# Attention generators advanced at one place of each weight chunk instead of two, and the closing spare products taken out

## The chip, the cores and the metric

The kernel runs on one core of one Trainium2 chip. The metric is the device time of one execution in microseconds (us); the time stated for a kernel is the median of several runs. Five engines work on the core side by side, each on its own queue in order: TensorE (PE in the profile; PEld is its weight load), VectorE (DVE), ScalarE (ACT), GpSimd (POOL) and SyncE (SP), which issues most of the DMAs. Products are written to PSUM, which has eight banks in each partition; ACT and DVE read them out.

## The reference

One inference step of a two-layer encoder for two groups of rows, 272 of a new stream (16 learned rows and 256 frames) and 32 of a running one with 128 cached rows. In each layer one projection feeds four mixers on the same normalised rows: A, multi-head latent attention; B, stick-breaking attention; C, differential attention; D, attention on the best keys that an indexer picks. Each mixer's output is projected, weighted by a sigmoid gate, summed and projected again; a squared-ReLU MLP follows.

```python
def _layer(x, ...):
    proj = jnp.einsum('bqd,de->bqe', x, w_in)          # feeds A, B, C, D and the gates
    ...
    score = jnp.einsum('bqh,bqhk->bqk', wi, jax.nn.relu(idx_s))    # D: the indexer
    _, sel = lax.top_k(score, topk)
    ...
    br = jnp.einsum('bqnw,nwd->bqnd', o, w_br)
    g = jax.nn.sigmoid(gates.reshape(bsz, nq, N_BRANCH, D_MODEL))
    mix = jnp.einsum('bqd,de->bqe', jnp.sum(g * br, axis=2), w_out)
    x = _layer_norm(DN_ALPHA * x + mix, ln1_g, ln1_b)
    h = jnp.square(jax.nn.relu(jnp.einsum('bqd,df->bqf', x, w_ff1) + b_ff1))
    x = _layer_norm(DN_ALPHA * x + jnp.einsum('bqf,fd->bqd', h, w_ff2) + b_ff2, ln2_g, ln2_b)
```

## The kernel before

The weights come as one stream of 128 x 1024 blocks in float32. The code calls the work on one block a step; here it is called a chunk. SP loads a block into `raw` (four buffers); `split` (L170) makes two parts of it, `whi` on ACT (L172) and the rest `wlo` (L174) on DVE or, for some chunks, on POOL (three buffers each); PE then makes 24 products of it, eight slices of rows by three (`whi` with `xh`, `whi` with `xl`, `wlo` with `xh`; L301 for the projection chunks, L177 to L179 for the others). A chunk's products are written in two halves of 12 by `st.mm(st, 0)` and `st.mm(st, 1)`. What reads a chunk's result out (`after`) is written at the end of the next chunk.

PE's order is the order in which the code is written. The order of ACT, DVE and POOL is made by a scheduler when the kernel is built. The results lie in two pools of PSUM: four single banks (`bank`, L67) for the chunks' results `fp` and for the small tiles `pw`, `vp`, `td`, `tp`, `uq` and others, and two pairs of banks (`bank2`, L64) for scores and values (`ix`, `sc`, `z`, `av`). The build gives each new tile one of its pool's banks, and the tile waits until the readers of the tile before it in that bank are done.

The attention work is in generators, started when a layer's chunks begin: `lane_v` (L342: value tiles, `vp`), `lane_d` (L513: mixer D's indexer: `pw`, `ix`, `td`, rounds of MAX8 and MATCH_REPLACE on DVE, then its scores), the chain of `lane_c` (L622), `lane_b` (L702) and `lane_a` (L837), and `lane_a0` (L779). The list `active` holds them. Once in a chunk each is advanced by one `next`, and writes a few small products and the work of the other engines behind them. Here the list is split: `lane(0)` advances the generators at even places before the chunk's first 12 products, `lane(1)` those at odd places between the two halves.

Names that come up later: `wiT` is the indexer's weights read out of the projection (L506), and `lane_d` begins with `pw` (L521), made of it. `kiT` (L499 to L502) are the indexer's keys. `BK` (L325, L326) and `gt` (L936) are read-outs of a chunk's `fp`, `VB` (L356, L357) that of a `vp` tile. `SEL` (L579) is the mask that the rounds end in; mixer D's score tiles `s` get it by an addition on POOL (L610) and are taken out of `sc` on DVE (L611). L186 to L188 are three steps of a reciprocal root on DVE. After the last chunk come the sums of the last normalisation (`st`, L1251 and L1253), then 80 products (L1260 to L1272) whose results nothing reads, and then the normalisation and the output.

Of the kernel before, what the change touches and what calls it, by code (L numbers as in the profile page):

```python
# [21 lines left out]
NM, NP, NS, NPAST = 16, 256, 32, 128  # L22
TP = NM + NP
T = TP + NS
# [28 lines left out]
def trunk(ctx: ExitStack, tc, I, O):  # L53
    nc = tc.nc
    PE, ACT, DVE, POOL, SP = nc.tensor, nc.scalar, nc.vector, nc.gpsimd, nc.sync
# [8 lines left out]
    def bank2(name):  # L64
        return ps.tile([128, 2, 512], F32, name=name, tag="at", bufs=2)

    def bank(name):  # L67
        return ps.tile([128, 512], F32, name=name, tag="mm", bufs=4)
# [40 lines left out]
    negb = cst.tile([128, 512], BF16, name="negb")  # L109
    identb = cst.tile([128, 128], BF16, name="identb")  # L110
    xh = cst.tile([128, KT, T + 2], F32R, name="xh")
# [54 lines left out]
    def load(st):  # L166
        st.raw = wp.tile([128, 1024], F32, name="raw", tag="raw", bufs=4)
        SP.dma_start(st.raw, I['w'][st.l, st.c])

    def split(st):  # L170
        st.hi = wp.tile([128, 1024], F32R, name="whi", tag="whi", bufs=3)
        ACT.activation(st.hi, st.raw, AF.Copy)  # L172
        st.lo_t = wp.tile([128, 1024], F32R, name="wlo", tag="wlo", bufs=3)
        st.lo.tensor_tensor(st.lo_t, st.raw, st.hi.bitcast(F32), OP.subtract)  # L174
# [960 lines left out]
    active = []  # L1135
    later = []
    queue = list(steps)
# [57 lines left out]
    def by_block(a, b, half):  # L1195
        for kt in range(4 * half, 4 * half + 4):
            for st in (a, b):
                for k in range(3):
                    st.one(st, kt, k)

    prev, pending = None, []
    for i, st in enumerate(queue):
        if i in first_of:
            l = first_of[i]
            if l:
                late[l] = norm[0]
            active = active + lanes_of[l]
        if i + 4 < len(queue):
            load(queue[i + 4])
        if i + 2 < len(queue):  # L1210
            split(queue[i + 2])

        def lane(k):
            for g in active[k::2]:
                try:
                    next(g)
                except StopIteration:
                    dead.append(g)
        dead = []
        if st.pre:  # L1220
            st.pre()
        both = prev is not None and prev.hold == 2
        lane(0)
        if both:
            by_block(prev, st, 0)
        elif st.hold != 2:
            st.mm(st, 0)
        if prev is not None and prev.hold == 1:
            prev.mm(prev, 1)
        lane(1)  # L1230
        if st.mid:
            st.mid()
        if both:
            by_block(prev, st, 1)
        elif not st.hold:
            st.mm(st, 1)
        active = [g for g in active if g not in dead]
        for f in later:
            f()
        later.clear()  # L1240
        if st.after:
            pending.append((i + st.lag, st))
        while pending and pending[0][0] <= i:
            s = pending.pop(0)[1]
            s.after(s)
        prev = st
    assert not active
    m = norm[0]
    p = [bank("st")[:, m.c0:T] for _ in range(2)]
    for i in (1, 0):  # L1250
        PE.matmul(p[i], ones, m.s[i][:, m.c0:], start=True, stop=False)  # L1251
    for i, last in ((0, m.rk(7)), (1, m.sq)):
        PE.matmul(p[i], ones, last, start=False, stop=True)  # L1253

    lastw, flat, n = queue[-1], xh.rearrange("p k t -> p (k t)"), T - NM
    qa, qb = bank2("qa"), bank2("qb")
    q = [qa[:, 0], qa[:, 1], qb[:, 0], qb[:, 1]]
    hi = lambda i: lastw.hi[:, 128 * (i % 8):128 * (i % 8) + 128]
    for i in range(12):
        PE.matmul(q[0][:, :n], hi(i), xh[:, i % 8, NM:T], start=i == 0, stop=True, skip_group_check=True)  # L1260
    for i in range(12):
        PE.matmul(q[1 + i % 2][:, :n], hi(i), xh[:, i % 8, NM:T], start=i < 2, stop=True, skip_group_check=True)
    for i in range(8):
        PE.matmul(q[3], hi(i), flat[:, 512 * (i % 4):512 * (i % 4) + 512], start=i == 0, stop=True,
                  skip_group_check=True)
    for i in range(24):
        r = slice(64 * (i % 2), 64 * (i % 2) + 64)
        PE.matmul(q[i % 2][:, :n], hi(i)[r], xh[r, i % 8, NM:T], start=i < 2, stop=True, skip_group_check=True)
    for i in range(12):
        PE.matmul(q[2][:, :n], identb, negb[:, :n], start=i == 0, stop=True, skip_group_check=True)  # L1270
    for i in range(12):
        PE.matmul(q[3][0:96, :n], hi(i)[:, 0:96], xh[:, i % 8, NM:T], start=i == 0, stop=True,  # L1272
                  skip_group_check=True)
    m.mu, m.rs = (s[:, m.c0:] for s in m.s)
    v, mm = (e_tile([128, T], k)[:, m.c0:] for k in ("v", "mm"))
    ACT.activation(mm, p[0], AF.Square)
# [6 lines left out]
    for n, kt in enumerate((0, 4, 1, 2, 5, 3, 6, 7)):  # L1283
        m.scale(kt, POOL if kt in (4, 5) else DVE)
        g, b = (vec[:, o + kt:o + kt + 1] for o in (m.g, m.b))
# [135 lines left out]
```

## Time and profile before

| | |
|---|---|
| median of 3 runs | 1102.08 us (1101.89 to 1102.54) |
| the profiled execution's own time | 1101.63 us |
| its span in the profile | 1099.8 us (1.8 us lie around it) |
| PE busy | 1053.5 us, 96% of the span |
| DVE, ACT, POOL busy | 781.8, 604.7, 490.9 us |
| chain of work that ended last | PE 68%, DVE 18%, issue 5%, ACT 4%, POOL 3% |
| granted TensorE clock, mean | 0.99 of full speed |

The profile shows one execution; times in its rows are microseconds from the start of the span. A row of the timeline gives the start, the duration, the engine, the line, the operation, the tile written and the tiles read, the shapes and the count; in brackets, how long the engine was idle before it and which engine, tile and line ended that. PE's products overlap, so the step from one start to the next, not the row's duration, is what a product costs in a row of products. A granted clock of 1.00 is 2.4 GHz and 0.50 is 1.2 GHz.

### The profile page before, as it was taken

How to read it: one execution, taken by the hardware profiler on the slowest of the kernel's cores; microseconds unless marked ns; L12 is line 12 of the kernel's file. 1: busy time of each engine (PE TensorE's matmuls, PEld its weight loads, DVE VectorE, ACT ScalarE, POOL GpSimd, SP SyncE). 2: the span in 40 equal slices, each digit the busy share in tenths (PEclk: the TensorE clock that was granted, in tenths of full speed). 3: DMA queues.
4: the chain of work that ended last, by engine and by line, in shares of the span. 5: the costliest groups of instructions: out<-in, count | busy, mean ns of one | idle time of the engine just before them, and what ended most of it. 6: DMA issues, size and time to landing. Idle time of an engine off the chain costs nothing.

```text
span 1099.8 us, 20415 instructions
## 1 busy us (share of the span) xinstructions
PE 1053.5 (96%) x7906; PEld 998.2 (91%) x7906; DVE 781.8 (71%) x1499; ACT 604.7 (55%) x1067; POOL 490.9 (45%) x359
## 2 busy tenths in 40 slices
PE   7899998999999999999988999899999999999998
PEld 6888887889999899999988888788999989999997
DVE  8948887435798988645578588873468998874444
ACT  5555566556454677533334545675645658763332
POOL 5364555642667632111142644656527683221122
PEclk9999998999999999999998999999999999999999
DMA  7654332334444354544443543333344535454531
GB/s 253 206 181 135 108 125 88 106 109 134 146 142 140 129 173 153 164 161 155 153 156 123 172 121 127 108 103 118 118 155 153 170 115 181 165 173 160 167 135 44
DMA packets 56562, 157.42 MB, mean 143 GB/s; under 512 B 8912, under 2 KB 20624, under 8 KB 56464
## 3 DMA queue, kind: packets, MB, share of 16 engines
q1 hardware_dynamic: 55888, 155.52, 43.4%
q8 instruction: 62, 1.02, 0.4%
q10 hardware_dynamic: 576, 0.59, 0.2%
q14 instruction: 36, 0.29, 0.1%
HBM read 150.02 MB, written 6.07 MB: 142 GB/s over the span
## 4 chain that ended last, share of the span: by engine, by line
PE 68%; DVE 18%; issue 5%; ACT 4%; POOL 3%; DMA 1%; SPq 0%; ACTq 0%; POOLq 0%; DVEq 0%
PE fp L301 23%; PE f L179 11%; PE f L177 11%; PE f L178 11%; DVE wlo L174 3%; POOL r L243 2%; PE av L464 2%; PE br L177 1%; PE br L179 1%; PE br L178 1%; DVE xl L214 1%; DVE xl L259 1%; ACT whi L172 1%; DVE r L1061 1%; DVE v L186 1%
## 5 line engine op out<-in xcount | busy, mean ns | idle before, releaser
L172 ACT ACTIVATE whi<-raw 128x1024 fp32r<-128x1024 f32 x272 | 286.9, 1055 | 267.3 <-PE f L178 112.1
L174 POOL TENSOR_TENSOR wlo<-raw,whi 128x1024 fp32r<-128x1024 f32 x96 | 232.8, 2428 | 219.2 <-ACT whi L172 205.8
L174 DVE TENSOR_TENSOR wlo<-raw,whi 128x1024 fp32r<-128x1024 f32 x176 | 247.9, 1408 | 101.1 <-ACT whi L172 100.7
L301 PE MATMUL fp<-xh,whi 128*128 128x304 f32 (+3 forms) x896 | 283.8, 318 | 11.0 <-DVE u L273 5.1
L301 PE MATMUL fp<-xl,whi 128*128 128x304 f32 (+3 forms) x896 | 272.6, 304 | 6.0 <-DVE xl L259 4.2
L301 PE MATMUL fp<-xh,wlo 128*128 128x304 f32 (+3 forms) x896 | 272.2, 304 | 1.2 <-DVE wlo L1155 0.9
L301 PEld LDWEIGHTS fp<-xh,whi 128*128 128x128 f32 x896 | 171.6, 192 | 28.5 <-issue 22.1
L301 PEld LDWEIGHTS fp<-xl,whi 128*128 128x128 f32 x896 | 172.0, 192 | 9.2 <-DVE xl L259 5.6
L301 PEld LDWEIGHTS fp<-xh,wlo 128*128 128x128 f32 x896 | 171.4, 191 | 2.3 <-DVE wlo L1155 1.5
L179 PE MATMUL f<-xh,wlo 128*128 128x306 f32 (+1 forms) x512 | 155.1, 303 | 5.0 <-DVE wlo L174 4.9
L177 PE MATMUL f<-xh,whi 128*128 128x306 f32 (+1 forms) x512 | 154.4, 302 | 0.0
L178 PE MATMUL f<-xl,whi 128*128 128x306 f32 (+1 forms) x512 | 153.4, 300 | 0.0
L179 PE MATMUL f<-ht,wlo 128*128 128x304 f32 (+1 forms) x512 | 153.1, 299 | 0.0
L177 PE MATMUL f<-ht,whi 128*128 128x304 f32 (+1 forms) x512 | 152.6, 298 | 0.0
L178 PE MATMUL f<-ht,whi 128*128 128x304 f32 (+1 forms) x512 | 152.3, 297 | 0.0
L1049 POOL TENSOR_TENSOR u<-u,nsum 128x304 f32<-128x304 f32 (+1 forms) x64 | 63.5, 996 | 113.3 <-DVE u L273 106.7
L179 PEld LDWEIGHTS f<-xh,wlo 128*128 128x128 f32 x512 | 96.5, 188 | 6.8 <-DVE wlo L174 6.8
L178 PEld LDWEIGHTS f<-xl,whi 128*128 128x128 f32 x512 | 96.9, 189 | 0.1
L177 PEld LDWEIGHTS f<-xh,whi 128*128 128x128 f32 x512 | 96.7, 189 | 0.1
L177 PEld LDWEIGHTS f<-ht,whi 128*128 128x128 f32 x512 | 96.3, 188 | 0.0
L178 PEld LDWEIGHTS f<-ht,whi 128*128 128x128 f32 x512 | 96.2, 188 | 0.0
L179 PEld LDWEIGHTS f<-ht,wlo 128*128 128x128 f32 x512 | 96.2, 188 | 0.0
(328 smaller groups left out, 1801.2 us busy)
## 6 DMA issues: line engine op xcount, KB each, us to landing
raw<-in_w SPq DMA_DIRECT2D x272, 512.0 KB, 3.5
x<-in_x SPq DMA_DIRECT2D x8, 152.0 KB, 4.1
raw<-in_w SPq DMA_DIRECT2D x4, 256.0 KB, 4.5
dscr<-tab SPq DMA_DIRECT2D x4, 167.5 KB
out_y<-r ACTq DMA_DIRECT2D x4, 144.0 KB
out_y<-r SPq DMA_DIRECT2D x4, 144.0 KB, 2.0
bc<-dscr SPq DMA_DIRECT2D x2, 272.0 KB, 3.0
out_dsk<-DK SPq DMA_DIRECT2D x4, 136.0 KB
```

What stands on the lines that cost most here:

```text
L172: ACT.activation(st.hi, st.raw, AF.Copy)
L174: st.lo.tensor_tensor(st.lo_t, st.raw, st.hi.bitcast(F32), OP.subtract)
L177: PE.matmul(out, st.hi[:, wcol], mh, start=start, stop=False)
L178: PE.matmul(out, st.hi[:, wcol], ml, start=False, stop=False)
L179: PE.matmul(out, st.lo_t[:, wcol], mh, start=False, stop=stop)
L186: DVE.scalar_tensor_tensor(v, v, -0.5, y, op0=OP.mult, op1=OP.mult)
L214: DVE.scalar_tensor_tensor(xl[:, kt, c0:T], r, g, xh[:, kt, c0:T].bitcast(F32), op0=OP.mult, op1=OP.subtract)
L243: i = eng.tensor_tensor(self.rk(kt), self.rk(kt), self.mu, OP.subtract)
L259: DVE.scalar_tensor_tensor(xl[:, kt, self.c0:T], self.rk(kt), b, h.bitcast(F32), op0=OP.add, op1=OP.subtract)
L301: PE.matmul(box['p'][:, w], (st.lo_t if k == 2 else st.hi)[:, 128 * kt:128 * kt + 128], (xl if k == 1 else xh)[:, kt, w], start=st.n == 0, ...
L464: PE.matmul(p[64 * half:64 * half + 64, j, a:b], vv, pp, start=i == 0, stop=True, skip_group_check=True)
L1049: POOL.tensor_tensor(u, u, n.rs, OP.mult)
```

## The change

In the main loop, `lane(0)` and `lane(1)` become one loop over all of `active` before the chunk's first half. Nothing is written between the halves any more, save for the few chunks that have a `mid`. The generators themselves, their number of turns and the chunks stay as they are. The 80 products behind the last sums go, with their two pairs of banks.

```diff
-        def lane(k):
-            for g in active[k::2]:
-                try:
-                    next(g)
-                except StopIteration:
-                    dead.append(g)
         dead = []
...
         both = prev is not None and prev.hold == 2
-        lane(0)
+        for g in active:
+            try:
+                next(g)
+            except StopIteration:
+                dead.append(g)
         if both:
             by_block(prev, st, 0)
         elif st.hold != 2:
             st.mm(st, 0)
         if prev is not None and prev.hold == 1:
             prev.mm(prev, 1)
-        lane(1)
         if st.mid:
             st.mid()
...
-    lastw, flat, n = queue[-1], xh.rearrange("p k t -> p (k t)"), T - NM
-    qa, qb = bank2("qa"), bank2("qb")
...
-    for i in range(12):
-        PE.matmul(q[0][:, :n], hi(i), xh[:, i % 8, NM:T], start=i == 0, stop=True, skip_group_check=True)
...
-    for i in range(12):
-        PE.matmul(q[3][0:96, :n], hi(i)[:, 0:96], xh[:, i % 8, NM:T], start=i == 0, stop=True,
-                  skip_group_check=True)
     m.mu, m.rs = (s[:, m.c0:] for s in m.s)
```

On PE, groups of small products that stand between two products of chunks go from 119 to 88 (15 fewer in the first layer, 16 in the second), and those inside a chunk from 43 to 1. The following pieces of the order show three places; the number behind a tile's name tells one tile from another.

PE where `lane_d` begins in the first layer, before the change: `pw` stands in the middle of chunk `fp_728`.

```order
L301 MATMUL fp_728<-xh_84,whi_613 128x304
L301 MATMUL fp_728<-xl_85,whi_613 128x304
L301 MATMUL fp_728<-xh_84,wlo_615 128x304
L521 MATMUL pw_741<-con_73,wiT_677 64x4 x8
L524 MATMUL pw_741<-con_73,wiT_677 32x2 x4
L553 MATMUL ix_757<-kiT_600,DQ_207 64x272 x4
```

The same place with the change (the chunk is now called `fp_753`, the one before it `fp_691`).

```order
L301 MATMUL fp_691<-xh_84,whi_580 128x304
L301 MATMUL fp_691<-xl_85,whi_580 128x304
L301 MATMUL fp_691<-xh_84,wlo_582 128x304
L521 MATMUL pw_728<-con_73,wiT_677 64x4 x8
L524 MATMUL pw_728<-con_73,wiT_677 32x2 x4
L553 MATMUL ix_744<-kiT_600,DQ_207 64x272 x4
L301 MATMUL fp_753<-xh_84,whi_613 128x304
```

`pw` and the first `ix` come 12 products earlier, directly behind the chunk before. In the second layer they move the same way.

PE six and a half chunks later, where a `BK` chunk ends, before the change; `td` stands 12 products further on, in the middle of `fp_1166`.

```order
L301 MATMUL fp_1113<-xl_85,whi_918 128x304
L301 MATMUL fp_1113<-xh_84,wlo_920 128x304
L355 MATMUL vp_1153<-con_73,vf_1145 128x128 x3
L406 MATMUL tp_1162<-con_73,e_872 96x128 x2
L301 MATMUL fp_1166<-xh_84,whi_996 128x304
```

The same place with the change (`fp_1120` for `fp_1113`, `fp_1170` for `fp_1166`).

```order
L355 MATMUL vp_1153<-con_73,vf_1145 128x128 x3
L567 MATMUL td_1162<-acc_931,con_73 128x208
L406 MATMUL tp_1166<-con_73,e_876 96x128 x2
L301 MATMUL fp_1170<-xh_84,whi_996 128x304
L301 MATMUL fp_1170<-xl_85,whi_996 128x304
```

`td` now stands ahead of the chunk. So three single banks are taken between the two chunks instead of two, and the build gives `fp_1170` the fourth, which `fp_1120` has just filled, with six small products between them. Before, `fp_1166` had the bank of a `tp` with 24 chunk products in between. The same happens at `fp_1456`, which gets the bank of `fp_1386`, the chunk before it, read out by `gt` (L936), with 12 small products between. Both places come again in the second layer.

POOL where mixer D's first masks are made, in the first layer, as a piece of the difference.

```order
 L492 TENSOR_TENSOR SEL<-SEL,t_681 32x304
-L174 TENSOR_TENSOR wlo<-raw,whi 128x1024 x20
+L174 TENSOR_TENSOR wlo<-raw,whi 128x1024 x19
 L610 TENSOR_TENSOR s<-bc_98,SEL 128x544
-L174 TENSOR_TENSOR wlo<-raw,whi 128x1024
+L174 TENSOR_TENSOR wlo<-raw,whi 128x1024 x2
```

The first L610 goes ahead of one split of weights; its own place on PE, that of `sc` L382, doesn't move, while the tiles `z` of `lane_b` and their work on ACT and DVE come 12 products earlier. On DVE the order there changes as follows.

```order
L186 SCALAR_TENSOR_TENSOR v_2005<-v_2005,y_2007 128x304
L187 TENSOR_TENSOR v_2005<-v_2005,y_2007 128x304
L611 TENSOR_TENSOR s_2056<-sc_2051,s_2056 128x544
L188 SCALAR_TENSOR_TENSOR y_2007<-v_2005,y_2007 128x304
L389 TENSOR_REDUCE mx_2059<-s_2056 128x2
L725 SCALAR_TENSOR_TENSOR t_1964<-z_1942,t_1964 128x512
```

That was before the change; with it:

```order
L725 SCALAR_TENSOR_TENSOR t_1951<-z_1929,t_1951 128x512
L186 SCALAR_TENSOR_TENSOR v_2005<-v_2005,y_2007 128x304
L611 TENSOR_TENSOR s_2056<-sc_2051,s_2056 128x544
L187 TENSOR_TENSOR v_2005<-v_2005,y_2007 128x304
L389 TENSOR_REDUCE mx_2059<-s_2056 128x2
```

L187 falls behind L611, and the second L725 of `lane_b` goes ahead of it.

## Rows read from the trace of the kernel before

**Rows 1.** The page: busy time of each engine with its share of the span and its instructions, and the chain of work that ended last, by engine.

```profile
PE 1053.5 (96%) x7906; PEld 998.2 (91%) x7906; DVE 781.8 (71%) x1499; ACT 604.7 (55%) x1067; POOL 490.9 (45%) x359
...
PE 68%; DVE 18%; issue 5%; ACT 4%; POOL 3%; DMA 1%; SPq 0%; ACTq 0%; POOLq 0%; DVEq 0%
```

**Rows 2.** The waits of PE over the whole span: the product that waited, then the engine, tile and line that it waited for; microseconds in total, times, the longest.

```profile
PE sc L382 <- DVE s L611: 4.9, 2, 3.1
PE fp L301 <- DVE VB L357: 4.5, 2, 2.3
...
PE rms L786 <- ACT lat L763: 3.2, 1, 3.2
...
PE fp L301 <- ACT PTP L410: 0.8, 1, 0.8
```

**Rows 3.** Stretches of the first layer's attention: the stretch, its length, then busy time and instructions of PE, PEld, DVE, ACT and POOL, the granted clock, the DMA share and GB/s.

```profile
110.00:120.00 10.00, 7.54 (x55) 6.50 (x62) 8.99 (x30) 3.34 (x13) 4.50 (x2) 0.83 0.24 80
120.00:160.00 40.00, 40.00 (x348) 36.33 (x348) 33.48 (x108) 25.45 (x49) 19.37 (x8) 1.00 0.41 130
```

**Rows 4.** The timeline of PE: the first products of two chunks in a row with nothing between them; the first product of a chunk that `vp` follows, and that `vp`; the first of 12 products that `sc` follows, and that `sc`.

```profile
35.42 0.30 PE L301 MATMUL fp<-xh,whi 128*128 128x306 f32 x1
...
38.83 0.30 PE L301 MATMUL fp<-xh,whi 128*128 128x306 f32 x1
...
87.98 0.39 PE L301 MATMUL fp<-xh,whi 128*128 128x304 f32 x1
...
91.42 0.49 PE L355 MATMUL vp<-con,vf 128*128 128x128 f32 x3
...
95.16 0.45 PE L301 MATMUL fp<-xh,whi 128*128 128x304 f32 x1
...
97.08 0.47 PE L669 MATMUL sc<-CK,CBQ 32*64 32x144 f32 x8
```

**Rows 5.** The timeline where `lane_d` begins, first layer: the first product of the chunk in whose middle `pw` stands, a split of weights on ACT, `wiT` on DVE, and `pw`.

```profile
59.04 0.31 PE L301 MATMUL fp<-xh,whi 128*128 128x304 f32 x1
...
59.15 1.06 ACT L172 ACTIVATE whi<-raw 128x1024 fp32r<-128x1024 f32 x1 [0.24 <-issue]
...
60.45 0.47 DVE L506 COPY wiT<-fp 32x304 f32<-32x304 f32 x1 [0.88 <-ACT kiT L501]
...
61.00 0.63 PE L521 MATMUL pw<-con,wiT 32*64 32x4 f32 x16
```

**Rows 6.** The same in the second layer: the chunk's first product, `wiT`, `pw`.

```profile
606.45 0.31 PE L301 MATMUL fp<-xh,whi 128*128 128x304 f32 x1
...
607.87 0.47 DVE L506 COPY wiT<-fp 32x304 f32<-32x304 f32 x1 [1.27 <-ACT kiT L501]
...
608.39 0.63 PE L521 MATMUL pw<-con,wiT 32*64 32x4 f32 x16
```

**Rows 7.** The timeline behind the `BK` chunk, whose last product starts at 91.28: the next chunk's first product on PE, a split of weights and `BK` on ACT, `td` on PE, and the rest of `BK` on DVE.

```profile
92.36 0.41 PE L301 MATMUL fp<-xh,whi 128*128 128x304 f32 x1 [0.23 <-DVE PT L435]
...
92.80 1.04 ACT L172 ACTIVATE whi<-raw 128x1024 fp32r<-128x1024 f32 x1
...
93.75 0.38 ACT L325 ACTIVATE BK<-fp 128x272 f32<-128x272 f32 x1
...
94.85 0.62 PE L567 MATMUL td<-acc,con 128*128 128x208 f32 x2 [0.54 <-ACT PT L433]
...
96.80 0.17 DVE L326 COPY BK<-fp 128x32 f32<-128x32 f32 x1
```

**Rows 8.** The timeline behind the `gt` chunk, whose last product starts at 110.52: the next chunk's first product, `gt` on DVE, and `td` on PE.

```profile
114.23 0.38 PE L301 MATMUL fp<-xh,whi 128*128 128x304 f32 x1 [2.19 <-DVE VB L357]
...
116.17 0.47 DVE L936 TENSOR_SCALAR gt<-fp 128x304 f32<-128x304 f32 x1
...
116.70 0.85 PE L567 MATMUL td<-acc,con 128*128 128x144 f32 x2 [0.27 <-DVE gt L936]
```

**Rows 9.** Two stretches in which the granted clock is 0.50, by the same view and columns as rows 3.

```profile
115.70:119.10 3.40, 3.13 (x13) 2.76 (x12) 3.32 (x10) 0.96 (x5) 2.37 (x1) 0.50 0.23 77
166.90:173.70 6.80, 5.83 (x25) 4.90 (x26) 6.02 (x15) 3.68 (x11) 4.39 (x3) 0.50 0.30 100
```

**Rows 10.** The timeline ahead of the first layer's longest wait: `SEL` on DVE, the addition of `SEL` and a split of weights on POOL, one step of `lane_b` on ACT, two steps on DVE, and the `sc` that waited on PE.

```profile
159.40 0.24 DVE L579 TENSOR_SCALAR SEL<-wk 128x160 f32<-128x160 f32 x1
...
162.49 1.82 POOL L610 TENSOR_TENSOR s<-bc,SEL 128x544 f32<-128x544 f32 x1
...
164.28 2.57 POOL L174 TENSOR_TENSOR wlo<-raw,whi 128x1024 fp32r<-128x1024 f32 x1
164.35 0.65 ACT L724 ACTIVATE t<-t 128x512 f32<-128x512 f32 x1
...
164.68 2.50 DVE L187 TENSOR_TENSOR v<-v,y 128x304 f32<-128x304 f32 x1
...
167.10 0.71 DVE L611 TENSOR_TENSOR s<-sc,s 128x544 f32<-128x544 f32 x1
...
167.87 0.97 PE L382 MATMUL sc<-DK,DQ 64*64 64x208 f32 x8 [3.10 <-DVE s L611]
```

**Rows 11.** The timeline of the end: the last group of the spare products on PE, and the last operation on ACT.

```profile
1093.30 1.84 PE L1272 MATMUL qb<-xh,whi 128*96 128x288 f32 x12
...
1095.54 0.63 ACT L1289 ACTIVATE r<-r,vec 128x288 f32<-128x288 f32 x1 [0.16 <-issue]
```

More of the change, by code (lines that the diff above doesn't have):

```diff
@@ L1253, in trunk @@
         PE.matmul(p[i], ones, last, start=False, stop=True)
-    lastw, flat, n = queue[-1], xh.rearrange("p k t -> p (k t)"), T - NM
-    qa, qb = bank2("qa"), bank2("qb")
-    q = [qa[:, 0], qa[:, 1], qb[:, 0], qb[:, 1]]
-    hi = lambda i: lastw.hi[:, 128 * (i % 8):128 * (i % 8) + 128]
-    for i in range(12):
-        PE.matmul(q[0][:, :n], hi(i), xh[:, i % 8, NM:T], start=i == 0, stop=True, skip_group_check=True)
-    for i in range(12):
-        PE.matmul(q[1 + i % 2][:, :n], hi(i), xh[:, i % 8, NM:T], start=i < 2, stop=True, skip_group_check=True)
-    for i in range(8):
-        PE.matmul(q[3], hi(i), flat[:, 512 * (i % 4):512 * (i % 4) + 512], start=i == 0, stop=True,
-                  skip_group_check=True)
[L1266 to L1271, printed above, removed]
-        PE.matmul(q[3][0:96, :n], hi(i)[:, 0:96], xh[:, i % 8, NM:T], start=i == 0, stop=True,
-                  skip_group_check=True)
     m.mu, m.rs = (s[:, m.c0:] for s in m.s)
```

## The prediction

> **What bounds the kernel now.** I read the page's shares and its chain of waits first: PE is busy for 96% of the span and holds 68% of the chain [rows 1]. So a microsecond that PE neither works nor can work is a microsecond of the result, almost anywhere. Then I asked what PE waits for [rows 2]. What matters here all lies in the two layers' attention, and most of it is ended by DVE: `sc` for L611 (4.9 us), `fp` for `VB` (4.5); `rms` waits 3.2 for ACT. Then the stretches [rows 3]: from 110 to 120 DVE is busy for 8.99 of 10 us and PE for 7.54; from 120 to 160 PE runs without a break (40.00 of 40) with DVE at 33.48; right behind, PE has the longest wait of the layer [rows 10]. So two regimes alternate. Where PE runs through, a saved product or break counts in full. Ahead of a wait that DVE ends, PE only arrives earlier and waits longer, and what counts is when DVE gets there. Last come the stretches at half clock [rows 9]: two of them follow right behind waits of PE, of 2.19 [rows 8] and 3.10 us [rows 10]. Half clock costs more than the wait: a stretch of 3.40 us at 0.50 is worth 1.7 at 1.00, so it loses 1.7; the one of 6.80 loses 3.4. Only the attention and the last 15 us can move, since elsewhere no generator is running.
>
> **The change, part by part.** The sum is made against the profiled execution, 1101.63 us, which is 0.45 under the median of 1102.08.
>
> *Fewer breaks on PE.* There are 31 fewer groups of small products between chunk products. A chunk with nothing between takes 38.83 - 35.42 = 3.41 us, so 12 products take 1.705 [rows 4]. A chunk up to a `vp` takes 91.42 - 87.98 = 3.44, which makes a break worth 0.03; 12 products up to an `sc` take 97.08 - 95.16 = 1.92, which makes it 0.21 [rows 4]. I take the middle, 0.12: 31 x 0.12 = 3.7 us. Nearly all of these breaks lie ahead of one of the waits [rows 2], where the gain is paid only as far as DVE comes earlier too. I count half, -1.9; the bounds are 0 and -31 x 0.21 = -6.5.
>
> *`pw` half a chunk earlier.* In the first layer `pw` now starts at 61.00, and `wiT`, which it reads, ends at 60.45 + 0.47 = 60.92 [rows 5]: nothing is spare. What makes `wiT` late is in the same rows: ACT splits weights at 59.15, just as a chunk ends on PE, and only then reads out the keys that release DVE. The order on ACT and DVE up to there is unchanged, and so is the chunk that they hang on. With the change PE comes to `pw` at 59.04 and must stand until 60.92; the 12 products that filled this time, 61.00 - 59.04 = 1.96, come afterwards. Less a break, that is +1.8. In the second layer it is 608.39 - 606.45 = 1.94, with `wiT` ending at 608.34 [rows 6]: +1.8 again, 3.6 in both.
>
> *The bank of `BK`.* Now the chunk behind the `BK` chunk starts at 92.36 in a bank that was filled long before, and `BK` is read out at leisure: on DVE until 96.97, 5.5 us after its products [rows 7]. With the change that next chunk takes the very bank of `BK`, so it starts when both read-outs are done. ACT splits weights first, into the buffer that the `BK` chunk has just let go (there are three): from 91.5, 1.04 and 0.38 for `BK`, then 0.17 on DVE [rows 7] give 93.1. Without the bank the chunk would start at 92.4: now 92.36, less the wait of 0.23, and a `td` more, 95.16 - 94.85 = 0.31 [rows 4, 7]. So +0.8 at least; at most 96.97 - 92.4 = 4.6, if DVE stays as late as it is. Off that come the 0.23 and 0.54 that are lost there now [rows 7]. DVE has its `BK` right behind `SEL` in the new order, earlier than before, so I take a value near the lower end: +1.0 a layer, 2.0 in both.
>
> *The bank of `gt`.* The same a few chunks on. Now 2.19 + 0.27 us are lost there, and `gt` ends at 116.64 [rows 8], 6 us after its chunk; 1.7 more goes at half clock [rows 9]. With the change the next chunk waits for `gt` instead of `VB`, from 112.0 (114.23 - 2.19); DVE has `gt` behind the last rounds and a `SEL`. Between 113 (everything relaxed) and 118 (as late as now, and one `SEL` later) I find no ground to choose, so I take no change here, with -2 and +4 as bounds for each layer.
>
> The waits for `pw` and `BK`, 5.6 us in both layers, stand ahead of this one, which DVE ends. What DVE does there hangs on PE only in part (it is busy 8.99 of 10). So about half is taken up by it: +2.8, with bounds 0 and +5.6.
>
> *`sc` behind L611.* POOL has L610 one split earlier. `SEL` ends at 159.64 but L610 runs from 162.49 to 164.31 [rows 10]; with POOL free it would end by 161.5. On DVE, L187 (2.50 us, until 167.18, beside POOL's split until 166.85) no longer stands ahead of L611, which starts at 167.10 now. But the second L725 does, and that waits for ACT's L724, which ends at 165.00 [rows 10]. An L725 and an L186 follow before L611; I put them at 1.1 us together (L611 itself, over more columns, takes 0.71 [rows 10]), and at 2.5 if POOL holds one of them as it holds L187 now: L611 starts at 166.1 to 167.5. Since `lane_b` runs 12 products (1.7 us) ahead, L724 may be that much earlier too. I take -1.0 for the first layer; the bounds are -6.5, if the wait goes and with it both half-clock stretches (3.1 + 3.4), and +1.7. In the second layer L187 stays ahead of L611 and an L728 joins it: no change, between -2 and +1.8.
>
> *The rest.* The wait of 0.8 us for `PTP` [rows 2] gets a group of `lane_b`'s products in front of it: -0.4, of 0 to -0.8. `rms` keeps its place and I leave its 3.2 us. The spare products run beside the last normalisation: the products end at 1095.14, ACT's last operation at 1096.17 [rows 11], and nothing reads their banks. Removing them: 0.
>
> The sum: -1.9 + 2.8 + 0 - 1.0 - 0.4 = -0.5, which gives 1101.1 us in the profiled execution and 1101.6 as a median. About 1101.5.
>
> **Rivals.**
> *A. New waits stand where products were (slower).* The mechanism is the read-out just in time: `pw` for `wiT`, and the chunks behind `BK` and `gt`. For it speaks that `wiT` has 0.08 us to spare; against it, that DVE may make PE wait a little later anyway. If nothing is taken up: 3.6 for `pw`, 2 x 1.7 for `BK`, two new half-clock stretches of 1.7 behind waits about as long as the one before 115.7 [rows 8, 9], less 1.9 for breaks: +8.5, 1110 us. It decides from the point where the wait before the chunk behind `gt` is no shorter than 2.2 us.
> The Trainium skill has a rule that speaks for this rival: "Perfetto Trace Analysis", section "Optimizing Tensor Performance", wants independent groups of products to rotate through different PSUM banks, so that reading one out overlaps the next one's products. By that rule both chunks that come back to the bank just filled lose the whole read-out; no run so far shows such a pair here, and 1110 would be its time.
>
> *B. The waits for DVE shrink (faster).* The work of `lane_c`, `lane_d` and `lane_b` starts half a chunk earlier, so DVE and ACT reach L611 earlier. For it: the order on POOL, and the 6.5 us of the 40 ahead in which DVE is idle, with 14.6 of ACT [rows 3]. If the `sc` wait falls by 2.6 and its half clock by 3.4, and `rms` by 1: -7, 1095 us.
>
> *C. It changes nothing.* DVE sets the end of each attention stage whatever PE does: 1102. The order does change in 31 places, so this can only be by absorption.
>
> **How the numbers follow.** Forecast 0.40, by itself 1098 to 1105; A 0.27; B 0.25; C 0.08. A measurement of this kernel can tell 0.2% (2.2 us) from no change, so faster ends at 1099.9 and slower begins at 1104.3. Faster: 0.24 from B and 0.08 from the forecast, 0.32. Slower: 0.26 from A and 0.05 from the forecast, 0.31. Same: 0.37. B by itself spreads from 1090 to 1099 and A from 1105 to 1113, by the bounds above; a range from 1093.5 to 1110 leaves out some 0.08 of B and 0.11 of A.
>
> **What would show it.** Right: `pw` waits about 1.9 us for `wiT` in both layers; the chunk behind `BK` waits 0.8 to 2 for it; the first layer's wait for L611 falls to about 2; from 1083 to the end nothing changes. Wrong: no wait at `pw` (then `wiT` hangs on something else); a half-clock stretch right behind `pw` (A); no half clock behind 160 (B); a chain that ended last with another share of DVE by some points; an end of the program that moves by more than 0.3 us, against the zero for the spare products.

## The result, and the profile after

The changed kernel takes 1118.23 us (median of 4 runs, 1114.0 to 1118.69) against 1101.99 for the kernel before: a ratio of 1.0138 [1.0113, 1.0163], 15 us slower. The profiled execution took 1118.65 us with a span of 1116.8, 17.0 longer than before. The forecast was 1101.5, no change, in a range up to 1110. Three runs further down were slow (1755.8 and 1267.17 us of two experiments, 2015.62 of the kernel before) and count in no ratio.

The page after, busy time and chain, as in [rows 1]:

```profile
PE 1047.2 (94%) x7822; PEld 995.5 (89%) x7826; DVE 788.2 (71%) x1499; ACT 604.3 (54%) x1067; POOL 489.3 (44%) x359
...
PE 67%; DVE 21%; issue 5%; ACT 4%; POOL 3%; DMA 0%; SPq 0%; POOLq 0%; ACTq 0%; DVEq 0%
```

The chain has 3 points more of DVE. PE has less to do (the spare products) and takes longer, so it waits. Its waits after, in the same view as [rows 2]:

```profile
PE sc L382 <- DVE s L611: 3.7, 2, 2.0
...
PE vp L355 <- ACT vf L336: 2.8, 2, 1.4
PE rms L786 <- ACT lat L763: 2.8, 1, 2.8
PE fp L301 <- DVE BK L326: 2.5, 2, 1.3
...
PE fp L301 <- DVE gt L936: 2.4, 2, 1.2
PE tp L406 <- DVE PT L435: 2.2, 2, 1.1
PE pw L521 <- DVE wiT L506: 1.9, 1, 1.9
PE tp L406 <- ACT QA L860: 1.9, 1, 1.9
PE pw L521 <- issue: 1.8, 1, 1.8
...
PE rms L798 <- POOL lat L775: 1.6, 1, 1.6
...
PE tp L406 <- DVE VB L357: 1.5, 2, 0.8
```

The longest waits of before are still there, a little shorter (`sc` 3.7 for 4.9, `rms` 2.8 for 3.2), but for that of `fp` for `VB`, which a `tp` now has (1.5 for 4.5). The other eight lines shown didn't exist before; four of them say "2 times", once in each layer, and `pw` has two lines, one for each layer. Five more of 0.6 to 1.2 us are new further down. All the waits of PE that are longer than 0.2 us come to 53.7 us in the span, against 41.1 before.

The start of the same chunk on PE in both traces shows where this becomes time. Up to the chunk behind `gt` the differences are made at three kinds of place:

| first product of | before | after | later by |
|---|---|---|---|
| chunk that waits for the first normalisation | 31.95 | 34.21 | 2.26 |
| chunk behind the new place of `pw` | 59.04 | 64.58 | 5.54 (of which 1.65 comes back within two chunks, as `ix` moved ahead) |
| chunk behind `BK` | 92.36 | 101.03 | 8.67 |
| chunk behind `gt` | 114.23 | 123.64 | 9.41 |
| output projection, first layer | 316.74 | 324.64 | 7.90 |
| second layer: chunk that waits for the normalisation | 578.55 | 586.50 | 7.95 |
| chunk behind the new place of `pw` | 606.45 | 617.93 | 11.48 |
| chunk behind `BK` | 639.77 | 655.95 | 16.18 |
| chunk behind `gt` | 661.63 | 677.41 | 15.78 |
| output projection | 851.21 | 868.27 | 17.06 |

Behind the chunk behind `gt` the delay swings, between 7.3 and 11.9 us in the first layer and between 13.9 and 19.1 in the second, and ends 1.5 lower and 1.3 higher.

The place behind `BK` in the first layer, in the timeline (compare [rows 7]): PE's three waits in a row, and what ACT and DVE did meanwhile.

```profile
88.80 2.51 DVE L651 SCALAR_TENSOR_TENSOR e<-s,rc 128x272 f32<-128x272 f32 x1
...
92.52 1.26 DVE L562 SCALAR_TENSOR_TENSOR acc<-rl,WI,acc 128x208 f32<-128x208 f32 x1
...
94.82 0.56 DVE L643 TENSOR_REDUCE mx<-s 128x2 f32<-128x416 f32 x1
95.41 0.47 ACT L646 ACTIVATE s<-s,mx 128x208 f32<-128x208 f32 x1 [4.46 <-DVE mx L643]
96.59 0.41 ACT L336 ACTIVATE vf<-fp 128x304 f32<-128x304 f32 x1
97.05 0.55 PE L355 MATMUL vp<-con,vf 128*128 128x128 f32 x3 [1.40 <-ACT vf L336]
98.88 0.41 DVE L435 COPY PT<-tp 112x256 f32<-112x256 f32 x1
99.34 0.42 PE L406 MATMUL tp<-con,e 128*96 128x128 f32 x2 [1.09 <-DVE PT L435]
100.79 0.18 DVE L326 COPY BK<-fp 128x32 f32<-128x32 f32 x1
101.03 0.62 PE L301 MATMUL fp<-xh,whi 128*128 128x304 f32 x1 [1.26 <-DVE BK L326]
```

`vp` waits for `vf`. Nothing is wrong with `vf` itself: on ACT it stands behind the exponentials L646, and ACT stood idle for 4.46 us until DVE had `mx`, which came behind L651 (2.51 us) and the indexer's L562 (1.26). Both ran while POOL made two splits of weights in a row, from 88.63 to 93.55; with POOL idle each took 0.42 on DVE, L562 at 94.12 and L651 at 97.91 (208 columns instead of 272). Before, POOL's splits stood apart here, at 87.88 and 93.92. Whether that pair is what makes `vf` late was not tested. Then `tp` waits for the bank that the `tp` before it has, and the chunk for the bank of `BK`. Each wait is short, and each is ended by a read-out that stands in its queue behind other work.

Behind `gt`, in the same trace (compare [rows 8]), `tp` waits for the bank of `VB` and the chunk for that of `gt`:

```profile
121.82 0.63 PE L406 MATMUL tp<-con,e 128*128 128x128 f32 x4 [0.66 <-DVE VB L357]
123.64 0.41 PE L301 MATMUL fp<-xh,whi 128*128 128x304 f32 x1 [1.20 <-DVE gt L936]
```

The stretches at half clock, in the same view as [rows 9]:

```profile
14.80:18.20 3.40, 3.40 (x15) 3.23 (x13) 2.52 (x7) 1.44 (x3) 1.33 (x3) 0.50 0.84 311
25.00:28.40 3.40, 3.40 (x13) 3.07 (x13) 1.97 (x8) 0.52 (x2) 0.00 (x0) 0.50 0.54 170
100.10:106.90 6.80, 5.88 (x23) 5.88 (x24) 4.29 (x19) 1.73 (x6) 0.55 (x1) 0.50 0.38 119
124.00:127.40 3.40, 3.40 (x16) 3.40 (x15) 2.70 (x14) 0.80 (x4) 1.58 (x1) 0.50 0.51 148
618.90:622.30 3.40, 3.40 (x15) 3.40 (x15) 1.38 (x2) 0.00 (x0) 1.04 (x2) 0.51 0.77 254
656.50:659.90 3.40, 3.40 (x15) 3.40 (x15) 2.92 (x11) 0.34 (x1) 0.00 (x0) 0.50 0.44 118
721.30:724.70 3.40, 3.40 (x16) 3.40 (x16) 3.40 (x4) 2.99 (x7) 3.40 (x3) 0.51 0.40 147
```

In the attention that is 6.80 + 4 x 3.40 = 20.4 us at half clock against 13.6 before (the 10.2 of [rows 9], and one more of 3.4 at 661.8 in the second layer), 3.4 us more lost. The stretch at 618.9 stands right behind `pw`, that at 100.1 behind `BK`. The two at 14.8 and 25.0 stand ahead of every moved product; they make the 2.26 us of the table's first line.

### The profile page after: what moved, and what is told of

Its sections match the earlier page's. It is cut to its first block, busy times and chain, and to the rows that moved or that the text cites. A ratio compares the mean times of both kernels' runs of the same rounds, so it can differ in the third digit from the quotient of the medians.

```text
span 1116.8 us, 20240 instructions
## 1 busy us (share of the span) xinstructions
PE 1047.2 (94%) x7822; PEld 995.5 (89%) x7826; DVE 788.2 (71%) x1499; ACT 604.3 (54%) x1067; POOL 489.3 (44%) x359
## 4 chain that ended last, share of the span: by engine, by line
PE 67%; DVE 21%; issue 5%; ACT 4%; POOL 3%; DMA 0%; SPq 0%; POOLq 0%; ACTq 0%; DVEq 0%
PE fp L301 23%; PE f L179 11%; PE f L177 11%; PE f L178 11%; DVE wlo L174 3%; POOL r L243 2%; PE av L464 1%; PE br L177 1%; PE br L179 1%; PE br L178 1%; DVE wk L576 1%; DVE r L1061 1%; DVE xl L259 1%; DVE xl L214 1%; DVE m L575 1%
## 5 line engine op out<-in xcount | busy, mean ns | idle before, releaser
L301 PE MATMUL fp<-xl,whi 128*128 128x304 f32 (+3 forms) x896 | 276.1, 308 | 5.9 <-DVE xl L259 4.2
L301 PE MATMUL fp<-xh,wlo 128*128 128x304 f32 (+3 forms) x896 | 275.6, 308 | 1.1 <-DVE wlo L1155 1.0
L301 PEld LDWEIGHTS fp<-xh,whi 128*128 128x128 f32 x896 | 174.6, 195 | 26.0 <-issue 15.2
L301 PEld LDWEIGHTS fp<-xl,whi 128*128 128x128 f32 x896 | 175.0, 195 | 9.0 <-DVE xl L259 5.5
L301 PEld LDWEIGHTS fp<-xh,wlo 128*128 128x128 f32 x896 | 174.7, 195 | 2.0 <-DVE wlo L1155 1.5
```

What stands on the lines that cost most here:

```text
L301: PE.matmul(box['p'][:, w], (st.lo_t if k == 2 else st.hi)[:, 128 * kt:128 * kt + 128], (xl if k == 1 else xh)[:, kt, w], start=st.n == 0, ...
```

## The experiments

Ratios are to the kernel before, run on the same chip in the same job; differences in us are the ratio's, at 1102 us.

### The generators alone, and the spare products alone

The first has the changed main loop and the 80 products; the second the loop of before and no spare products.

> The changed kernel with the 80 spare products put back: the move of the generators alone. Theory W (the new waits of PE and the half-clock stretches behind them, all in the attention, make the whole loss): 1114 to 1119 us, like the changed kernel. Theory S (the spare products matter for the clock at the beginning: the changed kernel has half-clock stretches at 14.8 and 25.0 us that the kernel before lacks, 2.3 us lost ahead of any moved product): 1111 to 1116 us, with no half clock before 60 us.

> The kernel before without the 80 spare products, generators at two places as before. Theory W: 1101.5 to 1102.5 us, no change. Theory S: 1103 to 1106 us, with half-clock stretches ahead of 30 us.

Measured: 1117.64 us, ratio 1.0139 [1.0124, 1.0155], for the generators alone; 1102.17 us, 1.0002 [0.9993, 1.0011], for the spare products alone. The generators make the whole loss and the spare products nothing: theory W. The half clock at the beginning comes of neither: the first kernel, which has the spare products, shows 3.4 us of it at 14.6 and again at 24.9, and the second, which hasn't, shows it too:

```profile
14.00:17.40 3.40, 3.16 (x13) 2.92 (x12) 2.90 (x6) 1.24 (x3) 1.23 (x3) 0.51 1.04 387
24.30:27.70 3.40, 3.11 (x10) 2.77 (x11) 1.72 (x8) 0.52 (x2) 0.00 (x0) 0.50 0.54 165
171.00:174.40 3.40, 3.40 (x16) 3.40 (x15) 3.31 (x10) 2.24 (x6) 1.28 (x1) 0.51 0.20 61
```

It has two stretches more there than the profiled execution of before, half as much behind its wait for L611, and the same median. So of the 17.0 us between the two profiled executions some two belong to these executions, not to the change. In what follows the kernel with the generators alone (1.0139, +15.3 us) is the one to compare with.

### Which generator

```diff
+        held = [g for g in active if g.__name__ == 'lane_d']
+        turn([g for g in active if g not in held])
...
             prev.mm(prev, 1)
+        turn(held)
```

> The changed kernel with the spare products, and mixer D's generator alone advanced in the middle of the chunk, all others at its start. Theory D (the generator of mixer D makes the loss: pw waits for wiT, td takes a single bank between two chunks): no wait at pw and none for BK, 1100 to 1106 us. Theory C (the chains of mixers C and B, half a chunk earlier or later, make it): 1110 us or more.

Measured: 1108.71 us, 1.0063 [1.0047, 1.0080], +6.9. More than half of the loss goes with mixer D's generator; up to the chunk behind `gt` this kernel's chunks start 2.4 us later than those of before, which all comes of the first 27 us, ahead of any moved product, and no chunk waits for `BK`. What is left is made later. Between the two theories: mostly D, with a part that isn't.

### All generators in the middle

The same loop as the changed one, written behind the first half instead of ahead of it.

> All generators at one place, but in the middle of the chunk, with the spare products. pw then stands where it stood before. Theory D1 (pw just in time is the larger part): 1100 to 1107 us. Theory D2 (three or more small tiles in a row use up the four single banks, so that the next products need the bank just filled, wherever the place is): 1110 to 1118 us, with waits for BK and gt as in the changed kernel, but none at pw.

Measured: 1131.49 us, 1.0262 [1.0246, 1.0277], +28.9, beyond both. `pw` doesn't wait here, but others do:

```profile
PE sc L382 <- DVE s L611: 11.7, 2, 6.6
PE tp L406 <- DVE BK L326: 6.6, 2, 3.4
...
PE vp L355 <- DVE VD L357: 3.0, 2, 1.5
...
PE td L567 <- DVE PT L435: 2.1, 2, 1.1
PE td L567 <- DVE gt L936: 1.8, 1, 1.8
```

So one place for all is expensive wherever it is, which speaks for D2.

### `pw` alone, and the bank of `td` alone

Two repairs of the changed loop, each by itself: mixer D's generator in the middle until `pw` is written, and `td` in a bank pair.

```diff
+        held = [g for g in active if g.__name__ == 'lane_d' and 'WI' not in g.gi_frame.f_locals]
+        turn([g for g in active if g not in held])
```

```diff
-                p = bank("td")
+                p = bank2("td")[:, 0]
```

> The changed kernel with the spare products, and mixer D's generator advanced in the middle of the chunk only until its pw is written, at the start from then on. Theory P (the wait at pw is paid in full in both layers: 3.3 us in the table of chunks less 1.7 won back by the moved products, and one half-clock stretch behind it): 1112 to 1115 us, no wait at pw, the waits behind the BK chunk as in the changed kernel. Theory A (waits that DVE ends take it up later): 1116 to 1118 us.

> The changed kernel with the spare products, and td in the pool of bank pairs instead of the single banks. Theory B (the chunk behind BK waits because td uses up the fourth single bank): no wait of fp for BK, 1110 to 1114 us. Theory Q (the read-outs come late because ACT and DVE have the score work of two mixers in a row in their queues; the bank is only the last of three waits there): vp and tp wait there as before and td adds a wait of its own, 1115 to 1120 us.

Measured: 1111.47 us, 1.0097 [1.0081, 1.0113], for `pw`: 4.6 us of the 15.3 go, theory P, just under its range. Nothing of it comes back behind `gt`: `VB` ends on DVE at 118.69 (121.67 in the changed kernel), `gt` at 120.61 (123.59), and the chunk behind it starts at 120.66 (123.64), all 2.98 us earlier. There DVE's read-outs follow PE. For `td` 1104.01 us, 1.0030 [1.0019, 1.0042]: 12.0 us go with one line that moves no product. The place behind `BK` in this kernel:

```profile
95.01 0.55 PE L355 MATMUL vp<-con,vf 128*128 128x128 f32 x3 [1.39 <-ACT vf L336]
95.39 0.52 PE L567 MATMUL td<-acc,con 128*128 128x208 f32 x2
95.75 0.38 PE L406 MATMUL tp<-con,e 128*96 128x128 f32 x2
97.30 0.41 PE L301 MATMUL fp<-xh,whi 128*128 128x304 f32 x1 [1.17 <-DVE PT L435]
```

Both theories had a part of it. The wait for `vf` is as long as before (1.39), as theory Q said: that is the queue on ACT. The waits of `tp` and of the chunk for `BK` go, as theory B said (the chunk still waits 1.17 for the bank of an older `tp`, that of `PT`), and so does the one for `gt`. The size speaks for B, and is larger than it said. Chunk by chunk against the generators alone, 1.7 us in each layer go at the chunk behind `BK`, 1.5 and 1.4 at the next one, 1.9 and 0.4 at the chunk behind `gt`: 8.6 together. Where the rest goes these two executions don't tell, as they differ in half clock elsewhere too. The stretch ahead of the chunk behind `gt`, by the view of [rows 3]:

```profile
105.00:115.00 10.00, 10.00 (x96) 9.27 (x96) 9.06 (x32) 5.11 (x15) 5.17 (x2) 1.00 0.34 107
```

And the timeline where it ends:

```profile
115.00 0.29 DVE L357 COPY VB<-vp 64x128 f32<-64x128 f32 x1
...
115.35 0.41 PE L301 MATMUL fp<-xh,whi 128*128 128x304 f32 x1
```

PE runs for 10.00 of 10 us with DVE at 9.06; in the ten microseconds of [rows 3] it was 7.54 with DVE at 8.99. That doesn't mean that DVE has time to spare here. The chunk behind `gt` has the bank of `VB` again, as before, and starts at 115.35, just when `VB` is read out (115.29). PE no longer stands because it comes later: the chunk ahead is 3.06 us later than before, this one 1.12, so 1.9 us are taken up. In the second layer the wait for `VB` goes from 2.34 to 0.94, and the delay from 1.50 to 0.99. In the changed kernel, where this chunk has the bank of `gt`, the same two are 9.46 and 9.41 later (15.85 and 15.77 in the second layer): nothing is taken up.

### Before and after the value generator ends

One kernel runs two places until `lane_v` ends and one from then on; the other the reverse.

> The kernel before (two places) as long as the value generator of a layer lives, the changed kernel (one place) from then on, with the spare products. Theory E (the loss is made in the first part of each layer's attention, at pw and behind BK): 1099 to 1104 us. Theory L (it is made later, around the scores of C, D and B): 1108 us or more.

> The reverse: one place as long as the value generator of a layer lives, two places from then on, with the spare products. Theory E: 1114 to 1119 us. Theory L: 1102 to 1108 us. If the two parts add up, the excess of this run and of the other makes 15 to 17 us.

Measured: 1105.07 us, 1.0034 [1.0020, 1.0048], +3.7, and 1125.77 us, the middle one of three runs that lie far apart, from 1116.59 to 1126.69, with a ratio of 1.0200 [1.0145, 1.0254], +22. The loss is made in the first part of the layer's attention (theory E), though both times lie above its ranges, by 1 and by 7 us, and the second time is uncertain. The parts do not add up: 3.7 and 22 are not 15.3. The one place late costs something by itself and gives something back where the one place early has gone before. Part of that is the clock: in the profile of the second kernel the later part of the first layer has the waits of the kernel before (3.10 for L611, 1.26 and 0.78 ahead of the chunk at 210.49), but then 10.24 us at half clock from 211.75, where the kernel before has none, and 4.6 us are lost there. What the rest comes of the runs don't show.

### Both repairs together, the second one without the change, and in the middle

> Both repairs at once: one place for all generators, but mixer D's advanced in the middle until its pw is written, and td in the pool of bank pairs; spare products kept. Theory P+B (the two costs are separate and add): 1104.0 less 3.3 for the waits at pw and 0 to 3.4 for the half clock behind them, 1097.5 to 1101 us. Theory R (a wait removed comes back at the next wait that DVE ends): 1102 to 1105 us.

> The kernel before with td in the pool of bank pairs: whether that move helps by itself. Theory B (single banks are short only where td, tp and vp stand in a row, which they don't here): 1099.5 to 1102.5 us, at most the 1.4 us that td waits there for PT and gt. If the whole gain of td's move is a gain of any order: 1090 to 1097 us.

> All generators in the middle of the chunk, td in the pool of bank pairs. Theory B: the waits of tp for BK (6.6 us), of td for PT and gt (3.9) and most of the half clock behind them go, 1110 to 1120 us from 1131.5. Theory L (the waits of sc for L611, 11.7 us there, and what they do to the clock make most of it): 1122 us or more.

Measured: both repairs 1101.99 us, 0.9992 [0.9980, 1.0003]; `td` in a pair in the kernel before 1102.41 us, 0.9998 [0.9988, 1.0009]; all in the middle with `td` in a pair 1121.0 us, 1.0171 [1.0152, 1.0190]. The repairs add (4.6 + 12.0 = 16.6; together, from 1.0139 to 0.9992, 16.2) and bring the changed loop back to where it started. The median lies between the ranges of the two theories; by the ratio it is 1101.1, at the edge of P+B. The pair is worth nothing without the change, so it is no gain in general. In the middle it is worth 10 us of 28.9, and the upper end of what theory B expected is just missed: there the waits for L611 (10.3 us) stay, and a chunk still waits for `BK` (2.5 us in all).

### A bank less, and no generator moved

```diff
-        return ps.tile([128, 512], F32, name=name, tag="mm", bufs=4)
+        return ps.tile([128, 512], F32, name=name, tag="mm", bufs=3)
```

> The kernel before with three single banks instead of four, nothing else: generators at two places, pw where it was. The chunk behind BK then takes the bank of the BK chunk with five small products between, as in the changed kernel, though no generator has moved. Theory B (shortage of single banks is what cost most): a wait of fp for BK of 1 to 4 us in each layer, 1106 to 1118 us. Theory Q (what costs is that the score work of two mixers comes in one burst, the banks follow): 1101 to 1105 us.

Measured: 1138.16 us, 1.0328 [1.0287, 1.0369], +36. Its waits of PE, the first rows:

```profile
PE fp L301 <- DVE u L273: 10.8, 2, 5.5
PE fp L301 <- DVE BK L326: 9.0, 2, 4.5
PE f L177 <- DVE u L273: 5.3, 2, 2.6
PE sc L382 <- DVE s L611: 5.0, 2, 3.1
PE fp L301 <- DVE gt L936: 4.3, 1, 4.3
```

The wait for `BK` appears, 4.5 us in each layer, in the program whose generators nobody has touched. It is larger than in the changed kernel, and the kernel also pays outside the attention (`u`, the normalisations), so its 36 us, beyond both ranges, are no measure of the change. But the mechanism stands by itself: one single bank is what keeps `BK` off PE's path.

## Why the prediction was wrong

- **The bank of `BK`: the step that failed.** It named the right place and the right bank, and took +1.0 us a layer between bounds of 0.8 (its own numbers, 93.1 - 92.4, give 0.7) and 4.6. The chunk behind `BK` came 4.6 us later in each layer (the chunk ahead of it was at 87.98 before [rows 4] and at 92.04 after, 4.06 later, and then 8.67; in the second layer 11.58 and then 16.18). That is the upper bound, but it came about in another way. I priced only the last of the three waits, for `BK` itself; its 1.26 is near the forecast by luck. `BK` was to be read out 1.6 us after its chunk, with ACT and DVE free; it took 5.3 (95.65 to 100.97), and only because two other waits held PE up did PE wait so little for it. These two I left out. That of `tp` for `PT` (1.09) comes of the same shortage, as `td` has the bank that `tp` then lacks; with `td` in a pair the chunk itself waits for `PT` (1.17) and nothing for `BK`, one bank wait instead of two. That of `vp` for `vf` (1.40) comes of the queues of ACT and DVE, and stays (1.39), and with it the chunk behind `BK` still comes 2.9 us later in each layer. The half clock right behind the place was not in the sum either.
- **The absorption: the other step that failed.** I let half of the waits be taken up by the one behind `gt`, which DVE ends. In the changed kernel nothing was, on balance: from the chunk behind `BK` to the one behind `gt` the delay went from 8.67 to 9.41, in the second layer from 16.18 to 15.78, and with the waits at `pw` removed 4.6 us went, with none of it lost again behind `gt`. The thought holds as long as the chunk waits for `VB`: with `td` in a pair that wait took up 1.9 us in the first layer and 0.5 in the second. But the change gives the chunk the bank of `gt`, the read-out of the chunk just ahead, and `gt` came 2.98 us earlier when PE did. The two terms for this place did not fit together: the one let a delay be taken up by a wait that the other replaced.
- **`pw`: right.** +1.8 a layer was forecast, and 1.81 and 1.86 us of wait stand there. The half clock behind it (618.9) came on top; it was held for possible and not in the sum. Removing it gave 4.6 us: both waits, 3.7 us, and some of the half clock.
- **The bank of `gt`: right in number.** No change was forecast, in bounds of -2 and +4; the wait of 2.19 became 0.66 and 1.20, and the chunk's delay moved by 0.7 and -0.4, from place to place. What it did to the absorption stands above.
- **`sc` behind L611: right in sign.** -1.0 was forecast in the first layer; the longest wait went from 3.10 to 2.0. In exchange `rms` waits 1.6 for POOL's `lat`. The half clock of 6.80 us behind it [rows 9] is gone in the changed kernel's profile, but with the generators alone 10.24 us stand there behind the same wait: from 156.82 to 192.67 of before the one wins 2.3 us and the other loses 2.4. What the term is worth can't be told from these.
- **Fewer breaks: not seen.** -1.9 was forecast. With both repairs in, the loop has nearly all of its 31 groups less and is at 0.9992 [0.9980, 1.0003], between 2.2 us faster and 0.3 slower. But this kernel still has waits that the kernel before lacks (1.4 for `vf` in each layer), so what the breaks are worth by themselves is not shown.
- **The rest.** `PTP` no longer waits (0.78), but there a `tp` waits 1.86 for `QA` (1.27 for a split before) and an `uq` 0.95 for `gt`, 2.81 for 2.05: the -0.4 was wrong in sign in this execution. The spare products: 0 forecast, 0 measured.
- **The signs.** All four signs of being right came out: 1.81 and 1.86 us at `pw`, 1.26 behind `BK`, 2.04 for L611, and an end that moved by 0.1 us. The time was wrong all the same, because they watched the places that were priced and not what stood ahead of them, nor whether a delay is taken up. Two signs against it came too: half clock right behind `pw` in the second layer, and 3 points more of DVE in the chain.
- **The rivals.** A is what happened: waits just in time, and half clock behind them. It had a chance of 0.27, and 1110 for its time was 7 to 8 us short, for the same reason as the forecast: it counted one wait at `BK`. Its deciding point was wrong too: the waits behind `gt` are shorter than 2.2 us together (1.86), and A happened all the same. The waits of B shrank by 1.6 us (`sc` from 4.9 to 3.7, `rms` from 3.2 to 2.8), far less than what the new ones cost. The Trainium skill's rule, in "Perfetto Trace Analysis", section "Optimizing Tensor Performance", that independent groups of products should rotate through different banks, is borne out by the bank experiments: 12.0 us for a tile moved to the other pool, 36 for a bank taken away.

What the runs leave open: why `vf` comes late on ACT, and why one place in the second part of a layer's attention costs 3.7 us by itself and seems to earn something after the first part has been delayed. No version was found that beats the kernel before.

## What to carry to other kernels

Small products that are put side by side to save breaks ask for their PSUM banks side by side too: count how many tiles of a pool are taken from one big product up to and with the next, and where that passes the pool's size, expect the product and the small ones ahead of it to stand for read-outs, and sum these waits. Before letting a later wait take up a delay, ask which read-out ends it, and whether that read-out hangs on the delayed engine. Here the wait for `VB` took up 1.9 us, and the wait for `gt`, the read-out of the chunk just ahead, took up nothing, with DVE busy for 9.06 of 10 us ahead of the one and 8.53 ahead of the other (115 to 125 us of the changed kernel).

## What was not expected of the hardware

Two programs that are the same up to the last 15 us (the kernel before, with and without the spare products) had different half-clock stretches in their profiled executions: none ahead of 100 us in the one, two of 3.4 us at 14.0 and 24.3 in the other, with the same waits of PE ahead of them (1.28 us for `xl` and 2.36 for the sums in the one, 1.28 and 2.37 in the other). Eleven of the profiled executions have the same order of instructions on PE, ACT and DVE up to 59 us: one, the kernel before, has no such stretch there, three have one of 3.4 us and seven have two. A half-clock stretch behind a wait is thus not a property of the program alone; single profiled executions can differ by some 2 us, and the medians agreed to 0.2.
In the changed kernel the wait of 1.86 us at `pw` in the second layer was followed by half clock (618.9), the one of 1.81 in the first layer was not. The wait of 2.04 to 2.05 for L611 in the first layer was followed by no half clock in the changed kernel, by 3.4 us with `pw` in the middle, 6.8 with `td` in a pair and 10.2 with the generators alone.
